# Parts of h, of the mixers' outputs and of the merged output at other places modulo 512 bytes

## The chip, the core and the metric

The kernel runs on one core of a Trainium2 chip, alone. The metric is the device time of one execution in microseconds, the median of several runs. A difference of two kernels is told as a ratio with its interval.

## What is computed

One decoder block on 256 positions of 2048 features, all float32: a normalised and modulated input, two causal mixers in parallel, a gated merge and an output projection.

```python
ada = c @ w_ada + b_ada
shift, scale, gate = jnp.split(ada, 3, axis=-1)
h = rms_norm(x, g_pre) * (1.0 + scale[:, None, :]) + shift[:, None, :]
proj = h @ w_in                                    # 2048 x 11824
(qa, kc, vc, ks, vs, kw, vw, ga, za, qb, kb, vb, zb, ma, mb) = jnp.split(proj, IN_SPLITS, axis=-1)
...
oa = nsa_attention(qa, ...)                        # 16 heads of 64, three branches
ya = (oa * jax.nn.silu(za)) @ w_br_a               # 1024 x 2048
...
ob = dilated_mixture(qb, kb, vb)                   # 8 heads of 128
yb = (ob * jax.nn.silu(zb)) @ w_br_b               # 1024 x 2048
merged = jax.nn.sigmoid(ma) * ya + jax.nn.sigmoid(mb) * yb
out = merged @ w_out                               # 2048 x 2048
return x + gate[:, None, :] * rms_norm(out, g_post)
```

## The kernel before, in words

Nearly all of the time goes into four products of float32 operands: h with w_in, the two mixers' outputs with w_br_a and w_br_b, and the merged output with w_out. Each is made of three products of parts. A float32 operand is split into a high part, rounded to fp32r, and a low part, the rest; the weights give wH and wL, h gives xH and xL, the mixers' outputs yH and yL, the merged output mH and mL. The product is high x high, high x low and low x high, summed in PSUM.

The weights come in items of up to 1024 columns per partition: one or two rows of 128 of the contraction (`kt`, 16 of them for h), 512 columns wide as a rule, 304 or 256 in a few panels. SP's queue loads an item into `raw` (seven buffers), ScalarE writes wH from it (L488), VectorE writes wL (L489), and TensorE multiplies. `items` is the order of the work, written out ahead: four passes over the panels of w_in as the rows of h become ready (PASSES and PIECES: row 0, rows 1 and 2, 3 to 6, 7 to 9, 10 to 12, 13 to 15), then the mixers' products and the output's. The attention of both mixers is a generator (`side_main`) of which a step is taken between items.

`product` (L528) issues an item's matmuls. For a panel as it is, the stationary operand is 128 columns (512 bytes per partition) of the h part and the moving operand the weights' 512 columns: for each of the item's rows L558 (xH with wH) and L559 (xL with wH), then for each row L561 (xH with wL), and the same for the second half of the positions. For the turned panels (za, zb) the weights are stationary and the h part, 256 columns, is moving: L548, L550, L553. The first pass uses unsplit float32 operands (L536, L540). Between these stand small matmuls of the attention and transposes; near the end two float32 rows of the gate are broadcast by products with a tile of ones, `ones_r` (L1146, L1147), and the compression of the first mixer takes loads of 128 and 64 columns in turn (L574, L575).

A tile's place in SBUF follows from the order in which the pools' tiles are made. The pool `const` comes first; a tile of 64 bytes that nothing uses (`align`) makes it end at a multiple of 512 bytes per partition. All tiles of the pools `big`, `wp` and most of `work` are multiples of 512 bytes long, so each begins at a multiple of 512: xH (16 rows in one tile), the six xL parts, the panels' tiles QA to ZB, whose places the mixers' outputs take over later, and the weights' tiles. mL takes the place of xH, the mH parts those of xL. Tiles of `const` begin anywhere at a multiple of 32: `ones_r` at 192 past a multiple of 512, VBD at 384.

Of the kernel before, what the change touches and what calls it, by code (L numbers as in the profile page):

```python
# [9 lines left out]
F32 = mybir.dt.float32  # L10
F32R = mybir.dt.float32r
BF = mybir.dt.bfloat16
I32 = mybir.dt.int32
AF = mybir.ActivationFunctionType
OP = mybir.AluOpType
# [3 lines left out]
S, D, N_IN = 256, 2048, 11824  # L19
KT = D // 128  # L20
# [6 lines left out]
PASSES = ((0, 1), (1, 3), (3, 7), (7, 16))  # L27
# [3 lines left out]
PIECES = (((1, 3),), ((3, 7),), ((7, 10), (10, 13)), ((13, 16),))  # L31
# [2 lines left out]
DA = (4, 6)  # L34
LAST = 3
ALIGN = 64
A_SCALE = 64 ** -0.5
B_SCALE = 128 ** -0.5

# [8 lines left out]
def _build(ctx, tc, x, c, positions, w_ada, b_ada, g_pre, g_post, w_in, pe_ck, pe_cv, w_ck1, w_ck2,  # L48
           w_cv1, w_cv2, w_br_a, w_br_b, w_out, out):
    nc = tc.nc  # L50
    V, A, T, G, DMA = nc.vector, nc.scalar, nc.tensor, nc.gpsimd, nc.sync
    const = ctx.enter_context(tc.tile_pool(name="const", bufs=1))
    big = ctx.enter_context(tc.tile_pool(name="big", bufs=1))
# [2 lines left out]
    psum = ctx.enter_context(tc.tile_pool(name="psum", bufs=1, space=PSUM))  # L56

    const.tile([128, ALIGN // 4], F32, name="align")

    def rows(ap2d, r0, nr, c0, n):  # L60
        return ap2d[r0 * 128:(r0 + nr) * 128, c0:c0 + n].rearrange("(a p) n -> p a n", p=128)
# [76 lines left out]
    rstd = const.tile([128, NT], F32)  # L138
    rsqrt(rstd, ssq, "x")

    xH = big.tile([128, KT, S], F32R, name="xH")
    hF = work.tile([128, PASSES[0][1], S], F32, name="hF", tag="PL", bufs=2)

    class Parts:

# [9 lines left out]
            tile_, a = self.at[k[1]]  # L155
            return tile_[k[0], k[1] - a, k[2]]

    groups = (PASSES[0],) + tuple(p for some in PIECES for p in some)
    xL, xT = Parts(), {}

    def lows(a, b, name, dt):
        return big.tile([128, b - a, S], dt, name=f"{name}{a}", tag=f"xL{a}")

    def x_norm(eng, a, b, t):
        xq = xs[:, t, a * 128:b * 128]
# [41 lines left out]
    AB = const.tile([128, 2, KT], F32)  # L207
# [10 lines left out]
    def make_h(a, b, acc):  # L218
        n = b - a
        if a:  # L220
            for half in range(2):
                ps = psum.tile([128, n, 128], F32, name="ada_ps", tag="pv")
                for j in range(n):
                    T.transpose(ps[:, j, :], acc[:, half, j * 128:(j + 1) * 128], ident)
                V.tensor_reduce(AB[:, half, a:b], ps, axis=AX.X, op=OP.add)
            V.tensor_tensor(AB[:, :, a:b], AB[:, :, a:b], bT[:, :, a:b], op=OP.add)
        else:
            V.tensor_tensor(AB[:, :, a:b], ada0[:, :, :, 0], bT[:, :, a:b], op=OP.add)
        V.scalar_tensor_tensor(AB[:, 1, a:b], AB[:, 1, a:b], 1.0, gT[:, a:b], op0=OP.add, op1=OP.mult)
        if a:  # L230
            h = ST[:, 2 + len(hxn) % 2].rearrange("p (k s) -> p k s", k=4)
        else:
            h = hF
        hxn.append(a)
        src = xT[a] if a else x0_ps
        if not a:
            for kt in range(b):
                ia = A.activation(xH[:, kt], src[:, kt], AF.Identity, scale=AB[:, 1, kt:kt + 1], bias=AB[:, 0, kt:kt + 1])
        for kt in range(a, b):
            V.tensor_scalar(h[:, kt - a], src[:, kt - a], AB[:, 1, kt:kt + 1], AB[:, 0, kt:kt + 1],  # L240
                            op0=OP.mult, op1=OP.add)
        if a:
            ia = A.activation(xH[:, a:b], h[:, :n], AF.Copy)
        low = lows(a, b, "xL", F32R)
        iv = V.tensor_tensor(low, h[:, :n], xH[:, a:b].bitcast(F32), op=OP.subtract)  # L245
        xL.put(low, a, b)
        return ia, iv

# [71 lines left out]
        tab["multB"], tab["maskB"], tab["keepC"], tab["maskC"], tab["blk"] = multB, maskB, keepC, maskC, blk  # L320


    QA = big.tile([128, NT, 1024], F32, name="QA", tag="qa")
    CV = big.tile([128, NT, 512], F32, name="CV", tag="cv")
    K2 = big.tile([128, NT, 4, 2, 64], F32, name="K2", tag="k2")
    VS = big.tile([128, NT, 256], F32, name="VS", tag="vs")
    VW = big.tile([128, NT, 320], F32, name="VW", tag="vw")
    ZA = big.tile([128, NT, 1024], F32, name="ZA", tag="za")
    QB = big.tile([128, NT, 1024], F32, name="QB", tag="qb")
    KB = big.tile([128, NT, 1024], F32, name="KB", tag="kb")  # L330
    VB = big.tile([128, NT, 1024], F32, name="VB", tag="vb")
    ZB = big.tile([128, NT, 1024], F32, name="ZB", tag="zb")
    MA = big.tile([128, NT, D], F32, name="MA", tag="ma")

    panels = []

# [364 lines left out]
    def side_main():  # L701
# [396 lines left out]

        while ("merged", 0) not in done:
            yield  # L1100
        mH, mL = Parts(), big.tile([128, KT, S], F32R, name="mL", tag="xH")
        for a, b in groups:
            mH.put(lows(a, b, "mH", F32R), a, b)
        yT["m"] = (mH, mL)
        for p in range(4):
            while ("merged", p) not in done:
                yield
            yield
            yield
            for t in range(NT):  # L1110
                ps = psum.tile([128, 4, 128], F32, name="m_ps", tag="pt")
                for j in range(4):
                    T.transpose(ps[:, j, :], MA[:, t, (4 * p + j) * 128:(4 * p + j + 1) * 128], ident)
                ts = slice(t * 128, (t + 1) * 128)
                for a, b in groups:
                    a, b = max(a, 4 * p), min(b, 4 * p + 4)
                    if a < b:
                        dH, o = mH.at[a]
                        A.activation(dH[:, a - o:b - o, ts], ps[:, a - 4 * p:b - 4 * p], AF.Copy, scale=0.5)
                        V.scalar_tensor_tensor(mL[:, a:b, ts], ps[:, a - 4 * p:b - 4 * p], 0.5,  # L1120
                                               dH[:, a - o:b - o, ts].bitcast(F32), op0=OP.mult, op1=OP.subtract)
                if t == NT - 1:
                    done.add(("mT", p))
                yield
# [105 lines left out]
```

## Time and profile before

| | |
|---|---|
| median of 3 runs | 824.94 us (823.79 to 826.5) |
| the profiled execution | 823.05 us |
| its span | 821.3 us |
| TensorE busy | 793.1 us, 97% |
| VectorE busy | 687.9 us, 84% |
| ScalarE busy | 417.7 us, 51% |
| GpSimd busy | 92.4 us, 11% |
| HBM read | 190.38 MB, 234 GB/s over the span |

The span is the time from the first to the last instruction of the profiled execution; its own time has a little before and behind it. Shares are of the span. In the rows PE is TensorE's matmuls, PEld its loads of stationary columns, DVE is VectorE, ACT ScalarE, POOL GpSimd. [...]

### The profile page before, as it was taken

The numbers are of one execution on the slowest core, as the hardware profiler recorded it, in microseconds if no ns is written. First come the engines' busy times: TensorE is split into PE (matmuls) and PEld (weight loads), VectorE is DVE, ScalarE is ACT, GpSimd is POOL, SyncE is SP. The second block draws the span as 40 slices with busy tenths as digits, with TensorE's granted clock in tenths as the row PEclk, the third lists the DMA queues.
The fourth block names the chain that finished last, engine by engine and source line by source line (L and its number), as shares of the span: only waits on it lengthen the run. The fifth ranks groups of instructions, "written<-read, shape, count | busy, mean of one in ns | idle before, by whom it ended". The sixth has DMA issues, their size and how long they took to land.

```text
span 821.3 us, 11929 instructions
## 1 busy us (share of the span) xinstructions
PE 793.1 (97%) x4160; PEld 667.3 (81%) x4160; DVE 687.9 (84%) x1068; ACT 417.7 (51%) x684; POOL 92.4 (11%) x111
## 2 busy tenths in 40 slices
PE   5999999999999999999999999999999999999995
PEld 4487888889887888888789999888887878888884
DVE  4799999999998879899888998867577999967455
ACT  2764263433434646566667666555644344445441
POOL 4200000000000026045412111001000010100000
PEclk9999999999999999999999999999999999999998
DMA  9899899999798547744444435655479999976533
GB/s 328 264 362 313 262 327 309 348 301 339 256 332 310 180 154 255 239 147 136 133 133 138 119 114 177 183 153 154 128 255 325 367 300 343 335 269 231 188 100 103
DMA packets 106950, 193.26 MB, mean 235 GB/s; under 512 B 7593, under 2 KB 36617, under 8 KB 106249
## 3 DMA queue, kind: packets, MB, share of 16 engines
q1 hardware_dynamic: 105376, 189.17, 69.5%
q10 hardware_dynamic: 1514, 3.33, 1.1%
q8 instruction: 33, 0.54, 0.3%
q14 instruction: 27, 0.22, 0.1%
HBM read 190.38 MB, written 2.10 MB: 234 GB/s over the span
## 4 chain that ended last, share of the span: by engine, by line
PE 85%; DVE 9%; issue 2%; DMA 2%; ACT 1%; DVEq 0%; ACTq 0%; SPq 0%
PE mm L558 21%; PE mm L561 21%; PE mm L559 21%; DVE wL L489 3%; PE mm L553 3%; PE mm L550 3%; PE mm L548 3%; PE mm L540 2%; DVE ST L509 2%; PE pt_ps L921 1%; PE sA L885 1%; PE ada_ps L183 1%; DMA xs<-in_x_dram 1%; DMA raw<-in_w_in_dram 1%; PE pvb_ps L1056 1%
## 5 line engine op out<-in xcount | busy, mean ns | idle before, releaser
L488 ACT ACTIVATE wH<-raw 128x1024 fp32r<-128x1024 f32 (+2 forms) x268 | 267.3, 1000 | 293.0 <-PE mm L559 182.3
L489 DVE TENSOR_TENSOR wL<-raw,wH 128x1024 fp32r<-128x1024 f32 (+2 forms) x268 | 316.4, 1185 | 74.1 <-ACT wH L488 69.2
L558 PE MATMUL mm<-wH,xH 128*128 128x512 f32 (+2 forms) x616 | 237.1, 387 | 1.3 <-DVE KB L631 1.1
L559 PE MATMUL mm<-wH,xL 128*128 128x512 f32 (+2 forms) x616 | 234.3, 382 | 0.0
L561 PE MATMUL mm<-wL,xH 128*128 128x512 f32 (+2 forms) x616 | 188.4, 383 | 0.4 <-DVE wL L489 0.4
L558 PEld LDWEIGHTS mm<-wH,xH 128*128 128x128 f32 x616 | 115.8, 188 | 23.0 <-issue 2.7
L559 PEld LDWEIGHTS mm<-wH,xL 128*128 128x128 f32 x616 | 115.9, 188 | 20.4 <-DVE xL L245 0.3
L561 PEld LDWEIGHTS mm<-wL,xH 128*128 128x128 f32 x616 | 113.1, 188 | 23.2 <-DVE wL L489 1.9
L509 DVE SCALAR_TENSOR_TENSOR ST<-raw,vecT,ST 128x768 f32<-128x768 f32 (+2 forms) x75 | 76.0, 1013 | 3.3 <-DMA raw<-in_w_ada_dram 3.1
L548 PE MATMUL mm<-xH,wH 128*128 128x256 f32 x240 | 63.5, 284 | 1.0 <-DVE VB L631 1.0
L550 PE MATMUL mm<-xL,wH 128*128 128x256 f32 x240 | 63.1, 283 | 0.0
L553 PE MATMUL mm<-xH,wL 128*128 128x256 f32 x240 | 50.0, 284 | 0.4 <-DVE wL L489 0.4
L558 PE MATMUL mm<-wH,yH 128*128 128x512 f32 x128 | 50.2, 392 | 0.0
L559 PE MATMUL mm<-wH,yL 128*128 128x512 f32 x128 | 50.0, 390 | 0.0
L558 PE MATMUL mm<-wH,mH 128*128 128x512 f32 x128 | 49.9, 390 | 0.0
L559 PE MATMUL mm<-wH,mL 128*128 128x512 f32 x128 | 49.9, 390 | 0.0
L548 PEld LDWEIGHTS mm<-xH,wH 128*128 128x128 f32 x240 | 45.9, 191 | 1.6 <-issue 1.6
L509 DVE SCALAR_TENSOR_TENSOR gacc<-raw,vecT,gacc 128x1024 f32<-128x1024 f32 x30 | 38.4, 1278 | 9.3 <-DMA raw<-in_w_ada_dram 9.3
L550 PEld LDWEIGHTS mm<-xL,wH 128*128 128x128 f32 x240 | 45.9, 191 | 0.0
L561 PE MATMUL mm<-wL,mH 128*128 128x512 f32 x128 | 39.8, 389 | 0.0
L561 PE MATMUL mm<-wL,yH 128*128 128x512 f32 x128 | 39.5, 390 | 0.0
L553 PEld LDWEIGHTS mm<-xH,wL 128*128 128x128 f32 x240 | 37.9, 192 | 0.8 <-DVE wL L489 0.8
(296 smaller groups left out, 1003.8 us busy)
## 6 DMA issues: line engine op xcount, KB each, us to landing
raw<-in_w_in_dram SPq DMA_DIRECT2D x165, 512.0 KB, 4.4
raw<-in_w_ada_dram SPq DMA_DIRECT2D x48, 512.0 KB, 5.5
raw<-in_w_ada_dram SPq DMA_DIRECT2D x48, 384.0 KB, 4.7
raw<-in_w_out_dram SPq DMA_DIRECT2D x32, 512.0 KB, 4.8
raw<-in_w_br_a_dram SPq DMA_DIRECT2D x16, 512.0 KB, 5.7
raw<-in_w_br_b_dram SPq DMA_DIRECT2D x16, 512.0 KB, 6.1
raw<-in_w_in_dram SPq DMA_DIRECT2D x29, 256.0 KB, 3.1
raw<-in_w_ada_dram SPq DMA_DIRECT2D x24, 256.0 KB, 4.9
```

What stands on the lines that cost most here:

```text
L183: T.matmul(ada0[:, half, j, :], lhsT=raws0[q][:, kk, half, j * 128:(j + 1) * 128], rhs=cT[:, kt:kt + 1].to_broadcast([128, 128]), start=(k ...
L488: A.activation(H, raw, AF.Copy)
L489: V.tensor_tensor(L, raw, H.bitcast(F32), op=OP.subtract)
L509: V.scalar_tensor_tensor(acc, r, cc, acc, op0=OP.mult, op1=OP.add)
L540: T.matmul(job.ps[t][:, :job.n], lhsT=hj[:, t * 128:(t + 1) * 128], rhs=it.raw[:, j, cs], start=(first and j == 0), stop=(last and j == it ...
L548: T.matmul(ps, lhsT=it.H[:, j, bs], rhs=sH[:, it.kt0 + j, :], start=(first and j == 0 and b == 0), stop=False, skip_group_check=True)
L550: T.matmul(ps, lhsT=it.H[:, j, bs], rhs=sL[:, it.kt0 + j, :], start=False, stop=False, skip_group_check=True)
L553: T.matmul(ps, lhsT=it.L[:, j, bs], rhs=sH[:, it.kt0 + j, :], start=False, stop=(last and j == it.nk - 1), skip_group_check=True)
L558: T.matmul(ps, lhsT=sH[:, it.kt0 + j, ts], rhs=it.H[:, j, cs], start=(first and j == 0), stop=False)
L559: T.matmul(ps, lhsT=sL[:, it.kt0 + j, ts], rhs=it.H[:, j, cs], start=False, stop=False)
L561: T.matmul(ps, lhsT=sH[:, it.kt0 + j, ts], rhs=it.L[:, j, cs], start=False, stop=(last and j == it.nk - 1))
L885: T.matmul(o, lhsT=QT[:, u.t, h // 2, h % 2, :], rhs=KTt[:, hl, :, 0:128] if u.t == 0 else KTt[:, hl, u.br, :], start=(hl == 0), stop=(hl ...
```

## The change

The single tile xH becomes six, one for each part of the rows of h, as xL was already; mL, which takes xH's place, likewise. `begin(offset)` makes an unused tile in the pool `big` that is just long enough for the next tile to begin `offset` bytes past a multiple of 512. Called ahead of each part it gives these places modulo 512:

| tiles | before | after |
|---|---|---|
| xH, xL, mH, mL, row 0 | 0 | 0 |
| rows 1 and 2 | 0 | 32 |
| rows 3 to 6 | 0 | 64 |
| rows 7 to 9 | 0 | 160 |
| rows 10 to 12 | 0 | 256 |
| rows 13 to 15 | 0 | 320 |
| QA, CV, K2, VS, VW, ZA, and in their places yH and yL of the second mixer, VR | 0 | 192 |
| QB, KB, VB, ZB, and in their places yH and yL of the first mixer | 0 | 224 |
| raw, wH, wL, and all else of `wp`, `work`; xs, MA, ST, AR, BS | 0 | 0 |

The unused tiles take 1536 bytes of each partition. The two programs have the same instructions with the same shapes in the same order on every engine, and each waits for the same; only addresses differ.

```diff
--- before.py
+++ after.py
@@ -34,6 +34,8 @@
 DA = (4, 6)
 LAST = 3
 ALIGN = 64
+OFFSETS = {0: 0, 1: 32, 3: 64, 7: 160, 10: 256, 13: 320}
+OFFSET_A, OFFSET_B = 224, 192
 A_SCALE = 64 ** -0.5
 B_SCALE = 128 ** -0.5
 
@@ -56,6 +58,15 @@
     psum = ctx.enter_context(tc.tile_pool(name="psum", bufs=1, space=PSUM))
 
     const.tile([128, ALIGN // 4], F32, name="align")
+    gaps = [0]
+
+    def begin(offset):
+
+        n = (offset - gaps[0]) % 512
+        if n:
+            big.tile([128, n // 4], F32, name=f"gap{len(gaps)}")
+            gaps.append(n)
+        gaps[0] = offset
 
     def rows(ap2d, r0, nr, c0, n):
         return ap2d[r0 * 128:(r0 + nr) * 128, c0:c0 + n].rearrange("(a p) n -> p a n", p=128)
@@ -138,8 +149,7 @@
     rstd = const.tile([128, NT], F32)
     rsqrt(rstd, ssq, "x")
 
-    xH = big.tile([128, KT, S], F32R, name="xH")
-    hF = work.tile([128, PASSES[0][1], S], F32, name="hF", tag="PL", bufs=2)
+    groups = (PASSES[0],) + tuple(p for some in PIECES for p in some)
 
     class Parts:
 
@@ -155,11 +165,31 @@
             tile_, a = self.at[k[1]]
             return tile_[k[0], k[1] - a, k[2]]
 
-    groups = (PASSES[0],) + tuple(p for some in PIECES for p in some)
+    def whole(name):
+        parts = Parts()
+        for a, b in groups:
+            if name == "xH":
+                begin(OFFSETS[a])
+            parts.put(big.tile([128, b - a, S], F32R, name=f"{name}{a}", tag=f"xH{a}"), a, b)
+        return parts
+
+    xH = whole("xH")
+    begin(0)
+    hF = work.tile([128, PASSES[0][1], S], F32, name="hF", tag="PL", bufs=2)
+
     xL, xT = Parts(), {}
 
+    seen = set()
+
     def lows(a, b, name, dt):
-        return big.tile([128, b - a, S], dt, name=f"{name}{a}", tag=f"xL{a}")
+        new = a not in seen
+        seen.add(a)
+        if new:
+            begin(OFFSETS[a])
+        part = big.tile([128, b - a, S], dt, name=f"{name}{a}", tag=f"xL{a}")
+        if new and b == KT:
+            begin(0)
+        return part
 
     def x_norm(eng, a, b, t):
         xq = xs[:, t, a * 128:b * 128]
@@ -235,14 +265,14 @@
         src = xT[a] if a else x0_ps
         if not a:
             for kt in range(b):
-                ia = A.activation(xH[:, kt], src[:, kt], AF.Identity, scale=AB[:, 1, kt:kt + 1], bias=AB[:, 0, kt:kt + 1])
+                ia = A.activation(xH[:, kt, :], src[:, kt], AF.Identity, scale=AB[:, 1, kt:kt + 1], bias=AB[:, 0, kt:kt + 1])
         for kt in range(a, b):
             V.tensor_scalar(h[:, kt - a], src[:, kt - a], AB[:, 1, kt:kt + 1], AB[:, 0, kt:kt + 1],
                             op0=OP.mult, op1=OP.add)
         if a:
-            ia = A.activation(xH[:, a:b], h[:, :n], AF.Copy)
+            ia = A.activation(xH.at[a][0], h[:, :n], AF.Copy)
         low = lows(a, b, "xL", F32R)
-        iv = V.tensor_tensor(low, h[:, :n], xH[:, a:b].bitcast(F32), op=OP.subtract)
+        iv = V.tensor_tensor(low, h[:, :n], xH.at[a][0].bitcast(F32), op=OP.subtract)
         xL.put(low, a, b)
         return ia, iv
 
@@ -320,17 +350,20 @@
         tab["multB"], tab["maskB"], tab["keepC"], tab["maskC"], tab["blk"] = multB, maskB, keepC, maskC, blk
 
 
+    begin(OFFSET_B)
     QA = big.tile([128, NT, 1024], F32, name="QA", tag="qa")
     CV = big.tile([128, NT, 512], F32, name="CV", tag="cv")
     K2 = big.tile([128, NT, 4, 2, 64], F32, name="K2", tag="k2")
     VS = big.tile([128, NT, 256], F32, name="VS", tag="vs")
     VW = big.tile([128, NT, 320], F32, name="VW", tag="vw")
     ZA = big.tile([128, NT, 1024], F32, name="ZA", tag="za")
+    begin(OFFSET_A)
     QB = big.tile([128, NT, 1024], F32, name="QB", tag="qb")
     KB = big.tile([128, NT, 1024], F32, name="KB", tag="kb")
     VB = big.tile([128, NT, 1024], F32, name="VB", tag="vb")
     ZB = big.tile([128, NT, 1024], F32, name="ZB", tag="zb")
     MA = big.tile([128, NT, D], F32, name="MA", tag="ma")
+    begin(0)
 
     panels = []
 
@@ -1098,7 +1131,7 @@
 
         while ("merged", 0) not in done:
             yield
-        mH, mL = Parts(), big.tile([128, KT, S], F32R, name="mL", tag="xH")
+        mH, mL = Parts(), whole("mL")
         for a, b in groups:
             mH.put(lows(a, b, "mH", F32R), a, b)
         yT["m"] = (mH, mL)
@@ -1117,7 +1150,7 @@
                     if a < b:
                         dH, o = mH.at[a]
                         A.activation(dH[:, a - o:b - o, ts], ps[:, a - 4 * p:b - 4 * p], AF.Copy, scale=0.5)
-                        V.scalar_tensor_tensor(mL[:, a:b, ts], ps[:, a - 4 * p:b - 4 * p], 0.5,
+                        V.scalar_tensor_tensor(mL.at[a][0][:, a - o:b - o, ts], ps[:, a - 4 * p:b - 4 * p], 0.5,
                                                dH[:, a - o:b - o, ts].bitcast(F32), op0=OP.mult, op1=OP.subtract)
                 if t == NT - 1:
                     done.add(("mT", p))
```

## Rows read from the trace of the kernel before

**Rows 1.** The page: busy us, share, instructions; TensorE's granted clock in 40 slices.
```profile
PE 793.1 (97%) x4160; PEld 667.3 (81%) x4160; DVE 687.9 (84%) x1068; ACT 417.7 (51%) x684; POOL 92.4 (11%) x111
...
PEclk9999999999999999999999999999999999999998
```

**Rows 2.** The page: the chain of work that ended last, by engine.
```profile
PE 85%; DVE 9%; issue 2%; DMA 2%; ACT 1%; DVEq 0%; ACTq 0%; SPq 0%
```

**Rows 3.** Groups by shape: out<-moving,stationary, count | busy us, mean ns | idle before.
```profile
L558 PE MATMUL mm<-wH,xH 128*128 128x512 f32 x556 | 220.4, 397 | 1.3 <-DVE KB L631 1.1
...
L548 PE MATMUL mm<-xH,wH 128*128 128x256 f32 x240 | 63.5, 284 | 1.0 <-DVE VB L631 1.0
```

**Rows 4.** Timeline of TensorE in the third pass: start us, us, operation.
```profile
301.55 0.39 PE L558 MATMUL mm<-wH,xH 128*128 128x512 f32 x1
...
305.63 0.39 PE L558 MATMUL mm<-wH,xH 128*128 128x512 f32 x1
```

**Rows 5.** Timeline of TensorE in a turned panel; ten matmuls are left out between.
```profile
501.72 0.28 PE L548 MATMUL mm<-xH,wH 128*128 128x256 f32 x1
...
503.04 0.28 PE L553 MATMUL mm<-xH,wL 128*128 128x256 f32 x1
```

**Rows 6.** Timeline, loads of 128 and 64 columns in turn; thirteen matmuls left out.
```profile
307.22 0.28 PE L574 MATMUL hid_ps<-wH,BS 128*128 128x256 f32 x1
...
308.86 0.28 PE L574 MATMUL hid_ps<-wH,BS 128*128 128x256 f32 x1
```

**Rows 7.** Timeline of the first pass's turned panels, and the group of their loads.
```profile
41.19 3.62 PE L536 MATMUL mm<-hF,raw 128*128 128x256 f32 x16
44.64 0.38 PE L224 MATMUL ada_ps<-ident,ST 128*128 128x128 f32 x2
...
L536 PEld LDWEIGHTS mm<-hF,raw 128*128 128x128 f32 x32 | 5.9, 190 | 1.1 <-issue 0.5
```

**Rows 8.** Groups of VectorE by shape: tiles that begin at 0 and at 384.
```profile
L631 DVE TENSOR_TENSOR KB<-mm,KB 128x512 f32<-128x512 f32 x12 | 7.9, 679 | 0.3 <-PE mm L561 0.3
...
L812 DVE TENSOR_TENSOR VBD<-vc_ps,blk 128x512 f32<-128x512 f32 x2 | 1.3, 680 | 0.0
```

**Rows 9.** Timeline of the panel of 304 columns; eleven matmuls left out.
```profile
141.03 0.30 PE L558 MATMUL mm<-wH,xH 128*128 128x304 f32 x1
...
142.71 0.30 PE L558 MATMUL mm<-wH,xH 128*128 128x304 f32 x1
```

**Rows 10.** Timeline around two gate broadcasts, matmuls, and two loads (PEld).
```profile
740.38 0.39 PE L558 MATMUL mm<-wH,mH 128*128 128x512 f32 x1
...
740.83 0.39 PE L558 MATMUL mm<-wH,mH 128*128 128x512 f32 x1
741.06 0.40 PE L1146 MATMUL g_ps<-gH,ones_r 128*128 128x512 f32 x1
...
741.99 0.39 PE L558 MATMUL mm<-wH,mH 128*128 128x512 f32 x1
...
742.66 0.40 PE L1147 MATMUL g_ps<-gL,ones_r 128*128 128x512 f32 x1
...
743.59 0.39 PE L558 MATMUL mm<-wH,mH 128*128 128x512 f32 x1
...
744.04 0.39 PE L558 MATMUL mm<-wH,mH 128*128 128x512 f32 x1
...
740.84 0.19 PEld L1146 LDWEIGHTS g_ps<-gH,ones_r 128*128 128x128 f32 x1
741.06 0.19 PEld L559 LDWEIGHTS mm<-wH,mL 128*128 128x128 f32 x1
```

**Rows 11.** Timeline of TensorE while attention is mixed in.
```profile
365.71 0.40 PE L558 MATMUL mm<-wH,xH 128*128 128x512 f32 x1
...
366.64 0.62 PE L561 MATMUL mm<-wL,xH 128*128 128x512 f32 x2
```

**Rows 12.** A stretch near the end: length, busy us of each engine, clock, DMA share.
```profile
760.00:800.00 40.00, 40.00 (x178) 33.14 (x177) 20.85 (x21) 19.77 (x25) 0.00 (x0) 1.00 0.46 146
```

## The prediction

> **What bounds the kernel now.** [...] The groups by shape show the stream: 556 matmuls each for L558, L559 and L561 with xH and xL at 512 columns, 240 each for the turned panels (L548, L550, L553) at 256 [rows 3]. With the mixers' and the merged operands the program has 2436 of 512 columns, 810 of 256 and 90 of 304, each with its own load of stationary columns: 3336 pairs.
>
> [...] From 301.55 to 305.63 us eighteen matmuls pass in 4.08 us: 226.7 ns each [rows 4]. At 256 columns eleven pass in 1.32 us, 120.0 ns each [rows 5]. [...] Where every other load has only 64 columns, fourteen matmuls of 256 take 1.64 us, 117.1 ns each [rows 6]: a quarter of the loaded columns less saves 2.9 ns, so a whole load costs about 11.6. [...] So the load and the moving stream, both read from SBUF, get in each other's way, at about 12 ns per load, 3336 x 12 = 40 us in all. That is the cost on which this change can act.
>
> **The change, part by part.** It moves no instruction: each engine has the same instructions with the same shapes and waits in the same order in both programs; only SBUF addresses differ. Before, every large tile begins at a multiple of 512 bytes, and since a stationary operand is 512 bytes wide, load and moving stream always begin at zero modulo 512. After, the weights still do, and the h, y and merged operands begin at 32, 64, 160, 192, 224, 256 or 320 past it. In 3264 of the 3336 pairs the two operands now stand apart.
>
> The side engines cost nothing. VectorE wrote VBD, which begins 384 bytes past a multiple of 512, in 680 ns for 128x512, and KB, which begins at zero, in 679 [rows 8]. The loads and stores whose place moves (about 260 on VectorE, 135 on ScalarE, 58 on GpSimd) keep their durations by that row, and only the matmuls are left.
>
> For these the trace has two rows with a nonzero place. The first is the item of 304 columns and two rows: its second row of weights begins 1216 bytes on, 192 past a multiple of 512, so the moving operand alternates between 0 and 192 against a load at zero. [...] The second is the gate broadcast, L1146 and L1147, whose stationary ones_r begins at 192, while its moving operand and all its neighbours are at zero. Before it the stream is in step: from 740.38 three matmuls take 0.68 us. From 741.06 four take 0.93 us, where 0.91 was due, though the load of the next one began on time, at 741.06 as well [rows 10]; then it is in step until 742.66, where the next such load stands, and again four take 0.93. From 743.59 two take 0.45, in step. A single load from another place throws the stream out of step, and finding it again costs 0.93 - 0.907 = 0.023 us. That is one change of place and one change back: about 11.5 ns per change.
>
> Counted over the dense matmuls in order, the place of the h operand against the weights' changes 541 times after the edit, because an item holds two of the 16 rows and several items (rows 0 and 1, 2 and 3, 6 and 7, 9 and 10, 12 and 13) span two parts. 541 x 11.5 ns = 6.2 us if each change costs that. Changes inside such an item follow each other after one or two matmuls, before the four are over, so the other way to count is by matmuls out of step: 666 within these items and some 130 x 4 behind them, at 23/4 = 5.8 ns each, 6.9 us. Against that, the stream is out of step already where attention is mixed in: from 365.71 four take 0.93 us [rows 11]; a change costs nothing new there. I take off about a quarter and keep **+5 us**, that is 823.05 + 5 = 828 on the profiled execution; on the median of 824.94, **830**.
>
> Bounds of this term: nothing (the 304-column row), and, if the stream never finds its step with operands apart, 5.8 ns on all 2436 wide matmuls, 14 us. Below nothing: whatever of the 12 ns per load goes away.
>
> **The rivals.** *The place does not matter* (time 825). [...] Against it: the two gate broadcasts, each with the same four late matmuls and no late load. They also differ from their neighbours in the tile that they write (g_ps), but the stream changes that with every item, without harm. [...]
>
> *Standing apart frees the load* (faster; this is the other side). The 12 ns may be paid because both operands begin at the same place modulo 512. If any place but zero avoids it, 3264 x 12 ns = 39 us go, 786. If one place in the list does, it decides by its share: 160, 256 and 320 carry 576 matmuls each, 7 us, 818; two of them 811. [...] For it: no row shows the other six places, and all 3336 loads now pay at the one place in use. It decides from the point at which about 430 loads are freed, which pays for the 5 us of lost step.
>
> *No step at all* (slower still): with operands apart the stream may never settle; 14 us, 839. [...]
>
> That the edit does not do what it says is excluded: the places of the built program are those of the list.
>
> **How the numbers follow.** A difference under 0.3%, 2.5 us, can't be told from none here. Lost step at each change, 830 (827.4 to 834): 0.34. No step at all, 834 to 842: 0.08. The place does not matter, 822.5 to 827.4: 0.33. Freed loads: 0.25, a little over half of it between 810 and 822.5, since one or two places are likelier than all. So faster 0.25, same 0.33, slower 0.42. The range 810 to 839 leaves out the far side of the freed loads (0.11) and the end of the no-step case (0.04), and holds some 0.85. The likeliest case has its own range, 827 to 834, beside it, as both signs carry weight.
>
> **What would show it.** In the changed kernel's trace the starts at one place: 226.7 ns in rows 7 and 8, 11, 14 and 15 of h, and 231 to 236 for about four matmuls behind each change, would confirm the lost step. A steady pace other than 226.7 at one place, which would stand out in the mixers' products (192 and 224 with no change for dozens of matmuls), would mean that the place itself sets the cost, and the sum above would be wrong in kind: below 226.7 the third case, above it the fourth. 226.7 through the mixed items too would be the second. The total of VectorE, ScalarE and GpSimd should stay as it is, and TensorE's clock too.

## The result and the profile after

The changed kernel takes 829.88 us (median of 5 runs, 828.9 to 831.23) against 825.69 us for the kernel before (5 runs, 823.79 to 826.5): slower, ratio 1.0074 with an interval of 1.0054 to 1.0095. The two medians alone are 4.2 us apart, a quotient of 1.0051, a little under the interval of the recorded ratio; in the 13 to 29 runs taken beside each batch of the experiments below the kernel before has medians of 823.3 to 824.3. The profiled execution has a span of 827.9 us, 6.6 more than before. One execution each of h_at_320 (991.8 us at a mean granted clock of 0.754, the one that was profiled) and of turned_320 (4520.5 us) stands far from all others of its kernel and is in no median below. The forecast of 830 us holds. The reason given for it does not: a change of place costs next to nothing (227.7 and 228.2 ns at the changes between 0 and 256 in one_part, 227.7 and 227.8 without one), and what sets the pace is where the two operands of a pair begin against each other (226.7 ns together, 233.3 with the weights alone moved in w_at_192).

The page of the kernel after, with the rows that answer to [rows 1] and [rows 2] (busy us, share, instructions; TensorE's granted clock in 40 slices; the chain of work that ended last by engine):

```profile
PE 799.4 (97%) x4160; PEld 664.4 (80%) x4160; DVE 689.4 (83%) x1068; ACT 417.5 (50%) x684; POOL 92.5 (11%) x111
...
PEclk9999999999999999999999999999999999999998
...
PE 77%; DVE 13%; DMA 5%; issue 2%; ACT 1%; DVEq 0%; ACTq 0%; SPq 0%
```

The count of instructions is the same, VectorE gained 1.5 us, ScalarE and GpSimd stand still, and the clock is granted as before. TensorE is busy 6.3 us longer, and still the largest share of the chain. The groups by shape, to hold against [rows 3] and [rows 8] (out<-moving,stationary, count | busy us, mean ns | idle before):

```profile
L591 PE MATMUL mm<-wH,xH 128*128 128x512 f32 x556 | 222.3, 401 | 1.3 <-DVE KB L664 1.0 <-ACT xH L273 0.3
...
L581 PE MATMUL mm<-xH,wH 128*128 128x256 f32 x240 | 62.7, 282 | 1.0 <-DVE VB L664 1.0
...
L664 DVE TENSOR_TENSOR KB<-mm,KB 128x512 f32<-128x512 f32 x12 | 7.9, 683 | 0.3 <-PE mm L594 0.3
...
L845 DVE TENSOR_TENSOR VBD<-vc_ps,blk 128x512 f32<-128x512 f32 x2 | 1.3, 680 | 0.0
```

L591 is the L558 of before, L581 the L548: the matmuls of 512 columns list 401 ns for 397, those of 256 list 282 for 284. So the wide ones became slower and the turned ones faster. The pace itself is read from starts: a listed 401 ns is longer than the 226.7 to 233.3 ns from one start to the next. In the timeline of TensorE (start us, us, operation) the mixers' products stand first, where every operand of one mixer keeps one place for 48 matmuls at a time: yH and yL of mixer A at 224, of mixer B at 192.

```profile
635.88 0.40 PE L591 MATMUL mm<-wH,yH 128*128 128x512 f32 x1
...
641.48 0.40 PE L591 MATMUL mm<-wH,yH 128*128 128x512 f32 x1
...
694.54 0.39 PE L592 MATMUL mm<-wH,yL 128*128 128x512 f32 x1
...
700.03 0.39 PE L592 MATMUL mm<-wH,yL 128*128 128x512 f32 x1
```

Twenty-four matmuls lie between the two rows of each pair. At 224 they take 5.60 us, 233.3 ns each; at 192 they take 5.49, 228.8 each. Before, the pace was 226.7 [rows 4]. There is no change of place in either stretch, and the stream never comes back to 226.7.

The narrower matmuls, eleven of the turned panel of [rows 5] and twelve of the panel of [rows 9], in the same timeline of the kernel after:

```profile
140.56 0.30 PE L591 MATMUL mm<-wH,xH 128*128 128x304 f32 x1
...
142.24 0.30 PE L591 MATMUL mm<-wH,xH 128*128 128x304 f32 x1
...
503.28 0.28 PE L581 MATMUL mm<-xH,wH 128*128 128x256 f32 x1
...
504.53 0.28 PE L586 MATMUL mm<-xH,wL 128*128 128x256 f32 x1
```

304 columns still take 140.0 ns. The turned panel went from 120.0 to 1.25 / 11 = 113.6 ns.

Where the time went, by the gaps between starts added up over the whole trace, from the 201st matmul on (the first 200 hold the waits of the start, of which the longest, for the DMA of g_pre, is 6.3 us before and 6.2 after): the matmuls of 512 columns, with the gaps behind them, took 560.3 us before and 570.3 after, +10.0; those of 256 and 304 columns took 114.4 and 113.1, -1.3; all others 77.8 and 77.7. Gaps under 243 ns behind a wide matmul, which hold no wait, had a mean of 227.8 ns (2306 of them) before and 232.3 (2315) after. The first 200 matmuls ended 1.9 us earlier than before, at 57.2 us for 59.1; in the kernels below this point lies between 57.0 and 58.5 (h_at_320 apart), so the profile of before was the late one, and this is not of the change. 10.0 - 1.3 - 0.1 - 1.9 = +6.7 us, which is the difference of the spans. Part of the 10.0 belongs to the same late start: three kernels below that keep the pace of before (one_part, h_at_256, turned_0) have their first 200 behind them at 57.9 to 58.1 and then take 561.8 to 562.2 us for the wide matmuls with their gaps. Against these three the change adds 8.1 to 8.5 us there, and 5.9 to 6.1 us to the span. The runs have it at 4.5 to 7.8 by the ratio's interval.

### The profile page after: what moved, and what is told of

The parts are those of the page before. It is cut to its first block, busy times and chain, and to the rows that moved or that the text cites. A ratio compares the mean times of both kernels' runs of the same rounds, so it can differ in the third digit from the quotient of the medians.

```text
span 827.9 us, 11929 instructions
## 1 busy us (share of the span) xinstructions
PE 799.4 (97%) x4160; PEld 664.4 (80%) x4160; DVE 689.4 (83%) x1068; ACT 417.5 (50%) x684; POOL 92.5 (11%) x111
## 4 chain that ended last, share of the span: by engine, by line
PE 77%; DVE 13%; DMA 5%; issue 2%; ACT 1%; DVEq 0%; ACTq 0%; SPq 0%
PE mm L592 20%; PE mm L591 20%; PE mm L594 20%; DVE wL L522 4%; DMA raw<-in_w_in_dram 3%; PE mm L586 3%; PE mm L583 3%; PE mm L581 3%; DVE ST L542 2%; PE pt_ps L954 1%; PE sA L918 1%; DMA xs<-in_x_dram 1%; ACT wH L521 1%; PE ada_ps L213 1%; PE pvb_ps L1089 1%
## 5 line engine op out<-in xcount | busy, mean ns | idle before, releaser
L591 PE MATMUL mm<-wH,xH 128*128 128x512 f32 (+2 forms) x616 | 239.0, 390 | 1.3 <-DVE KB L664 1.0
L594 PE MATMUL mm<-wL,xH 128*128 128x512 f32 (+2 forms) x616 | 190.5, 386 | 0.2 <-DVE wL L522 0.2
L591 PEld LDWEIGHTS mm<-wH,xH 128*128 128x128 f32 x616 | 115.7, 188 | 25.0 <-issue 2.5
L594 PEld LDWEIGHTS mm<-wL,xH 128*128 128x128 f32 x616 | 113.3, 188 | 24.6 <-DVE wL L522 0.7
L581 PE MATMUL mm<-xH,wH 128*128 128x256 f32 x240 | 62.7, 282 | 1.0 <-DVE VB L664 1.0
L591 PE MATMUL mm<-wH,yH 128*128 128x512 f32 x128 | 50.7, 396 | 0.0
L591 PE MATMUL mm<-wH,mH 128*128 128x512 f32 x128 | 50.6, 395 | 0.0
L581 PEld LDWEIGHTS mm<-xH,wH 128*128 128x128 f32 x240 | 45.2, 188 | 1.6 <-issue 1.6
```

Source lines behind the costliest of these rows:

```text
L581: T.matmul(ps, lhsT=it.H[:, j, bs], rhs=sH[:, it.kt0 + j, :], start=(first and j == 0 and b == 0), stop=False, skip_group_check=True)
L591: T.matmul(ps, lhsT=sH[:, it.kt0 + j, ts], rhs=it.H[:, j, cs], start=(first and j == 0), stop=False)
L594: T.matmul(ps, lhsT=sH[:, it.kt0 + j, ts], rhs=it.L[:, j, cs], start=False, stop=(last and j == it.nk - 1))
```

## The experiments

From here on the **relation** of a pair is the place at which its load (the stationary operand) begins, minus that of the moving operand under which it is read (that of the matmul which is listed as running when the load starts, as in [rows 10]), modulo 512 bytes. Theories: A, as forecast, a change of place costs about 11.5 ns. B, the place sets the pace, at each matmul. Within B: it is the operand's own place, or it is the relation. A stream of 512 columns is called in step at 226.7 ns. The ratio of each kernel is to the kernel before, run beside it.

**h_at_320: no change of place at all.** Against the kernel after:

```diff
-OFFSETS = {0: 0, 1: 32, 3: 64, 7: 160, 10: 256, 13: 320}
-OFFSET_A, OFFSET_B = 224, 192
+OFFSETS = {0: 320, 1: 320, 3: 320, 7: 320, 10: 320, 13: 320}
+OFFSET_A, OFFSET_B = 320, 320
```

> All parts of h, of the mixers' outputs and of the merged output begin at 320 modulo 512, the weights at zero: operands stand apart everywhere, and no change of place remains. If each change of place costs (the term of my prediction), the stream is in step: 226.7 ns per 512-column matmul, 120 per 256-column one, 825.7 us. If the place itself sets the pace, as the groups at 320 in the changed kernel suggest (233.2 ns at 512 columns, 115.4 at 256 in those pairs where the stationary begins 192 past the moving operand): 2346 x 5.5 ns = +13 us and 785 x -4.4 ns = -3.5 us, 835 us.

831.0 us (median of three; ratio 1.0088, 1.0057 to 1.0119); its trace is not read for the pace. The time alone is enough against A, which asked for 825.7: with every change of place taken from the wide pairs the cost did not fall. The 835 that B asked for was not reached either; w_at_192 shows why.

**all_at_64: everything away from zero, the weights too, nothing apart.** Against the kernel before:

```diff
-ALIGN = 64
+ALIGN = 128
```

> The kernel before with its unused tile 64 bytes longer: every large tile, weights included, begins at 64 modulo 512. If the place of one operand against the other counts: 226.7 ns, 825.7 us. If the distance of a tile's own beginning from a multiple of 512 counts: some 233 ns as at 64 in the changed kernel, +10 us or more, 836 us. If changes of place cost: 825.7 us.

825.12 us, ratio 1.0017 (1.0002 to 1.0032): at most 2.6 us, where the change under study costs 4.5 at least. Twenty-four matmuls of the mixers' products in its timeline:

```profile
633.27 0.39 PE L558 MATMUL mm<-wH,yH 128*128 128x512 f32 x1
...
638.71 0.39 PE L558 MATMUL mm<-wH,yH 128*128 128x512 f32 x1
```

5.44 / 24 = 226.7 ns. An operand's own place, tried at 64, costs nothing in the pace as long as both stand there together.

**w_at_192: only the weights move**, so the wide pairs have relation 320, the turned ones 192. Against the kernel before, with a tile behind it that gives later tiles their old places back:

```diff
+    work.tile([128, 80], F32, name="back", tag="back", bufs=1)
...
+    wp.tile([128, 48], F32, name="gap", tag="gap", bufs=1)
```

> h and all other parts at zero, wH and wL at 192 modulo 512. The places of the two operands against each other are those of the run with h at 320 (stationary minus moving is 320 in the wide panels, 192 in the turned ones). If only the relation counts: that run's paces (233 and 115 ns) and time, 835 us. If the stationary operand's own place counts: the wide panels, whose stationary h stays at zero, keep 226.7 ns, and only the turned panels change, 822 to 826 us. If changes cost: 825.7 us.

830.85 us, ratio 1.0074 (1.0051 to 1.0097), as slow as the change under study. The same twenty-four matmuls, timeline of this kernel:

```profile
635.51 0.39 PE L560 MATMUL mm<-wH,yH 128*128 128x512 f32 x1
...
641.11 0.39 PE L560 MATMUL mm<-wH,yH 128*128 128x512 f32 x1
```

5.60 / 24 = 233.3 ns, with h, y and merged at zero throughout. Together with all_at_64 this leaves the relation. It also shows A's failure in a clean profile: nothing changes place from pair to pair, and the wide stream is slow from one end to the other.

The time is 4 us under the 835 expected, and the gaps tell where that went. The wide ones without a wait grew from 227.8 to 233.3 ns, 13 us over 2397 of them. But the wide matmuls with all their gaps take 570.6 us, only 8.4 to 8.8 more than in one_part, h_at_256 and turned_0: beyond the pace their gaps hold 11.2 us of waiting here, and 15.7 to 16.1 there. That fits a stream that, being slower, reaches later what it waits for; it was not traced wait by wait. The matmuls of 256 and 304 columns give back another 2.0 us.

**scan_b: the other places.** Against the kernel after:

```diff
-OFFSETS = {0: 0, 1: 32, 3: 64, 7: 160, 10: 256, 13: 320}
-OFFSET_A, OFFSET_B = 224, 192
+OFFSETS = {0: 0, 1: 96, 3: 128, 7: 288, 10: 352, 13: 384}
+OFFSET_A, OFFSET_B = 480, 448
```

> As the changed kernel, with the places that it left out: 96, 128, 288, 352 and 384 for the rows of h and the merged operand, 480 and 448 for the mixers' outputs. If the place sets the pace, each has its own steady value at 512 and at 256 columns between 224 and 240 and between 112 and 122 ns, and the mixers' products (144 matmuls or more at one place) do not settle at 226.7: 827 to 836 us. If changes cost: 226.7 ns within each place, slower matmuls only behind a change, 830 us.

830.62 us, ratio 1.0074 (1.0048 to 1.01). Mixer A at 480 and mixer B at 448, timeline:

```profile
637.09 0.39 PE L591 MATMUL mm<-wH,yH 128*128 128x512 f32 x1
...
642.69 0.39 PE L591 MATMUL mm<-wH,yH 128*128 128x512 f32 x1
...
694.94 0.39 PE L592 MATMUL mm<-wH,yL 128*128 128x512 f32 x1
...
700.43 0.39 PE L592 MATMUL mm<-wH,yL 128*128 128x512 f32 x1
```

233.3 ns at 480 and 228.8 at 448: what 224 and 192 had given, 256 bytes further on. The means of the wide gaps without a wait, by relation, from this kernel and the one under study:

| relation | mean ns | relation + 256 | mean ns |
|---|---|---|---|
| 32 | 232.8 | 288 | 232.9 |
| 64 | 233.3 | 320 | 233.2 |
| 96 | 233.4 | 352 | 233.9 |
| 128 | 232.7 | 384 | 232.5 |
| 160 | 233.0 | | |
| 192 | 230.0 | 448 | 229.0 |
| 224 | 233.2 | 480 | 233.2 |

The table takes the gaps at which the place does not change. The mean of 230.0 at 192 hides two paces: mixer B's four stretches of 48 matmuls in the kernel under study run at 228.9 ns, but for the second, which runs at 233.3 at the very same places (at 448 all four run at 229.0):

```profile
670.61 0.40 PE L591 MATMUL mm<-wH,yH 128*128 128x512 f32 x1
...
676.21 0.40 PE L591 MATMUL mm<-wH,yH 128*128 128x512 f32 x1
```

Twenty-four matmuls take 5.60 us. So at 192 the relation takes the stream out of step, but does not alone fix the pace that it then has.

So it looked as if places count modulo 256. But 256 itself had shown 230.3 in the kernel after, and zero 231 there, between stretches at other places.

**one_part and h_at_256: is 256 as good as zero, and do changes between the two cost anything?** Against the kernel after, one_part and then h_at_256:

```diff
+OFFSETS = {0: 0, 1: 0, 3: 0, 7: 0, 10: 256, 13: 0}
+OFFSET_A, OFFSET_B = 0, 0
...
+OFFSETS = {0: 256, 1: 256, 3: 256, 7: 256, 10: 256, 13: 256}
+OFFSET_A, OFFSET_B = 256, 256
```

> Rows 10 to 12 of h and of the merged operand begin at 256 modulo 512, all other parts and all weights at zero. If the place sets the pace and the step is found again behind it: the stream returns to 226.7 ns within some five matmuls after each visit to those rows; 576 of 3336 pairs at 230 ns (396 of them wide) plus some 20 ns for each return, 826.5 to 828.5 us. If each change of place costs 11.5 ns and the place nothing: 226.7 ns inside rows 10 to 12 as soon as four matmuls have passed. If once apart the stream stays out of step: 231 ns in the other rows too, 830 us or more.

> All parts of h, of the mixers' outputs and of the merged output at 256, weights at zero. If the relation counts modulo 256: as before, 226.7 and 120 ns, 824 us. If it counts modulo 512 and the run with one part at 256 only kept a step found at zero: 230 ns at 512 columns as at 256 in the changed kernel, 828 to 830 us.

one_part: 824.17 us, ratio 1.0003 (0.9986 to 1.0021). h_at_256: 823.59 us, ratio 1.0000 (0.9988 to 1.0011). Timelines, one_part in the output's product where items pass between 0 and 256, then h_at_256 in the mixers':

```profile
760.01 0.39 PE L592 MATMUL mm<-wH,mL 128*128 128x512 f32 x1
...
765.45 0.39 PE L592 MATMUL mm<-wH,mL 128*128 128x512 f32 x1
```

```profile
633.11 0.39 PE L591 MATMUL mm<-wH,yH 128*128 128x512 f32 x1
...
638.55 0.39 PE L591 MATMUL mm<-wH,yH 128*128 128x512 f32 x1
```

Both are 24 matmuls in 5.44 us, 226.7 ns. one_part has 167 changes of place among its wide pairs; the gaps at them average 227.7 and 228.2 ns, those without a change 227.7 and 227.8. Theory A asked for 11.5 more. Modulo 256 holds for the wide stream at every place tried, and the 230.3 of relation 256 in the kernel after came from its neighbours, not from its place. h_at_256 is also the control for the edit itself: it has the six tiles in place of one and the unused tiles, and takes the time of the kernel before.

**one_part_64: the same changes, to a place that is not a multiple of 256.** One number differs from one_part:

```diff
-OFFSETS = {0: 0, 1: 0, 3: 0, 7: 0, 10: 256, 13: 0}
+OFFSETS = {0: 0, 1: 0, 3: 0, 7: 0, 10: 64, 13: 0}
```

> The run with one part at 256, with that part at 64 instead: the same changes of place at the same matmuls, only the place differs. If the relation modulo 256 sets whether the stream can be in step: 230 to 236 ns in the wide matmuls of rows 10 to 12, four or five late ones behind each visit, then 226.7 again; 396 x 5 ns = 2 us plus some 1.5 us behind the visits, 826.5 to 828.5 us, where 256 gave 824.2. If that run was in step because one part in six is too little to lose it: 226.7 here too, 824 us.

824.55 us, ratio 1.0024 (1.0008 to 1.0039); its span is 823.8 us for one_part's 821.8. The time is 2 us under the range expected, the paces are those expected. This kernel shows both effects side by side, in the third pass where rows 10 to 12 end and row 13 begins:

```profile
299.71 0.39 PE L591 MATMUL mm<-wH,xH 128*128 128x512 f32 x1
...
302.04 0.63 PE L594 MATMUL mm<-wL,xH 128*128 128x512 f32 x2
...
303.20 0.39 PE L592 MATMUL mm<-wH,xL 128*128 128x512 f32 x1
...
305.24 0.39 PE L591 MATMUL mm<-wH,xH 128*128 128x512 f32 x1
```

From 299.71 to 302.04 ten matmuls take 2.33 us, 233 each: at relation 64 the pace stays there and does not recover. The second matmul of the row at 302.04 starts at 302.27 and reads under it the first load at zero again. From there four matmuls take 0.93 us, the very figure of the gate broadcasts [rows 10], and then nine take 2.04, 226.7 each. So a return to zero costs some 0.02 us, and staying at 64 costs over 6 ns on every matmul. Where an item mixes 64 and zero, the returns come before the four are over, and the zero pairs pay as well: the 83 wide gaps at a change back to zero average 232.3 ns, the 298 at 64 without a change 233.4.

**low_at_64: as many changes as can be made.** Only xL and the mH parts stand at 64; xH, mL and y at zero. Against the kernel after:

```diff
+OFFSETS = {0: 64, 1: 64, 3: 64, 7: 64, 10: 64, 13: 64}
+OFFSET_A, OFFSET_B = 0, 0
...
-                begin(OFFSETS[a])
+                begin(0)
```

> Only the tiles that lows() makes (xL, and mH, which takes their places) begin at 64, everything else at zero; every third load stands apart, and the place changes with nearly every matmul. If a change costs 11.5 ns: some 2000 changes, +20 us, 845 us. If the place sets the pace and only pairs that stand apart pay: a third of the wide matmuls at 233, +5 us, 829 us. If one load apart is enough to keep the stream out of step: all wide matmuls between 230 and 236 ns, 832 to 836 us.

827.3 us, ratio 1.0042 (1.0024 to 1.0059), with some 2000 changes by the count that gave the forecast its 541, more than three and a half times as many, and a little over half of the cost. In the output's product, where the two places alternate:

```profile
763.61 0.39 PE L591 MATMUL mm<-wH,mH 128*128 128x512 f32 x1
...
767.79 0.39 PE L591 MATMUL mm<-wH,mH 128*128 128x512 f32 x1
```

18 matmuls in 4.18 us, 232.2 ns each, a change at two of three: not more than a steady place apart costs. In this product two of three loads stand apart (mH), with h only every third (xL); yet the wide gaps average 231.3 ns over the h products too, and those at a return to zero 232.5. So pairs at zero pay with their neighbours, as the last of the three cases had it: the next visit comes before four matmuls have passed. The time stayed under all three cases.

**y_at_224: the price of one place by itself**, h and merged at zero:

```diff
+OFFSETS = {0: 0, 1: 0, 3: 0, 7: 0, 10: 0, 13: 0}
+OFFSET_A, OFFSET_B = 224, 224
```

> h and the merged operand at zero; only the panels' tiles, and in their places the mixers' outputs, begin at 224. The 768-column share of the stream is 384 wide matmuls in one stretch with no change of place among them. If the place sets the pace: 233 ns there against 226.7, 384 x 6.5 ns = 2.5 us, 826.3 to 828 us, and 226.7 elsewhere. If changes cost: 226.7 ns everywhere, 823.8 us. The other engines' work on these tiles (attention, rotary, gates) adds nothing in either.

825.34 us, ratio 1.0014 (1.0000 to 1.0028), 1 us under the range expected. The wide gaps at 224 average 233.3 ns, all others 227.9. 377 gaps at 5.4 ns more are 2.0 us, and the span, at 824.1, lies 2.1 above h_at_256's. Runs alone would hardly tell so much from nothing.

**turned_0, turned_192, turned_320: can the faster turned panels be had alone?** The weights' tiles are made 128 columns longer, and the turned panels' weights begin 0, 192 or 320 bytes into them. To make room, one tile of `const` moves into `work` and a pool of four buffers has three (turned_0 is the control with that alone):

```diff
+            o = 48 if it.kind == "w" and it.jobs[0].turned else 0
-            H, L = (wp.tile([128, 1024], F32R, name="w" + x, tag="w" + x, bufs=3)[:, :it.nk * it.n].rearrange(
+            H, L = (wp.tile([128, 1152], F32R, name="w" + x, tag="w" + x, bufs=3)[:, o:o + it.nk * it.n].rearrange(
```

(48 words for turned_192; 0 and 80 in the other two.)

> A control for the next two runs: the kernel before, with wH and wL tiles 512 bytes longer (a tile of the identity's making and one of four rotary buffers give up their room), all operands at zero as before. 120 ns at 256 columns, 226.7 at 512; within 0.3% of the kernel before.

> As the control, but in the turned panels (za, zb: the weights are stationary, h moves) the weights lie 192 bytes into their longer tiles; the wide panels keep every operand at zero. If a pair's own place sets its pace: wide matmuls in step at 226.7, the 720 turned ones at 115 to 117 ns as in the two runs that had this relation, 720 x 3 to 4.5 ns = 2 to 3.3 us less than the control, 0.3 to 0.4% faster than the kernel before. If places apart only cost: as the control or slower.

> As the run with 192, with the weights of the turned panels 320 bytes into their tiles. The narrow panel of 256 columns ran at 115.1 ns at this relation with the weights shifted, the turned ones at 117.8 in the changed kernel with h at 192 or so; 115 to 118 ns expected, 1.5 to 3.5 us less than the control if a pair's own place sets its pace, nothing if places apart only cost.

824.2 us (ratio 0.9998, 0.9981 to 1.0015), 823.11 us (0.9985, 0.9971 to 1.0000) and 823.41 us (median of eleven; 0.9994, 0.9977 to 1.0011). The panel of [rows 5] in turned_0, then in turned_320:

```profile
500.85 0.28 PE L549 MATMUL mm<-xH,wH 128*128 128x256 f32 x1
...
502.17 0.28 PE L554 MATMUL mm<-xH,wL 128*128 128x256 f32 x1
```

```profile
499.41 0.28 PE L549 MATMUL mm<-xH,wH 128*128 128x256 f32 x1
...
500.66 0.28 PE L554 MATMUL mm<-xH,wL 128*128 128x256 f32 x1
```

Eleven take 1.32 us, 120.0 ns each, and 1.25 us, 113.6. Over the trace the gaps of 256 columns that hold no wait have a mean of 119.8 ns in turned_0, 117.2 at 192 and 115.4 at 320: over some 700 of them about 1.9 and 3.0 us saved. The wide ones keep their 227.8. The means are again mixtures of two paces. turned_192 runs two stretches of its turned panels, with the same places, like this:

```profile
473.14 0.28 PE L549 MATMUL mm<-xH,wH 128*128 128x256 f32 x1
...
477.22 0.28 PE L549 MATMUL mm<-xH,wH 128*128 128x256 f32 x1
...
490.68 0.28 PE L549 MATMUL mm<-xH,wH 128*128 128x256 f32 x1
...
494.92 0.28 PE L549 MATMUL mm<-xH,wH 128*128 128x256 f32 x1
```

Thirty-six matmuls take 4.08 us in the first, 113.3 ns each, and 4.24 in the second, 117.8. At 320 more of the stretches run at 113.3.

But the time does not follow clearly: the interval of turned_320 leaves no room for 3 us, that of turned_192 has room for its 1.9. The turned panels run among the attention, where TensorE waits for VectorE. Its waits from 430 to 500 us, turned_0, then turned_320 (engine line waited for: us in total, times, longest):

```profile
PE pt_ps L922 <- DVE AR L848: 0.7, 1, 0.7
PE pt_ps L922 <- DVE AR L834: 0.5, 1, 0.5
```

```profile
PE pt_ps L922 <- DVE AR L848: 1.0, 1, 1.0
PE pt_ps L922 <- DVE PL L927: 0.9, 1, 0.9
PE pt_ps L922 <- DVE AR L834: 0.6, 1, 0.6
PE pt_ps L922 <- DVE CS L871: 0.2, 1, 0.2
```

1.5 us more of waiting for producers that are no earlier: the waits of L922 for AR end 0.9 us sooner in turned_320, whose 201st matmul starts 1.0 us sooner. Half of the gain of 3.0 us ends there. In this profile the rest, and more, is lost later, between the mixers' products. Timeline of turned_320, and its stretch 665.0 to 668.5 us (length, busy us of each engine, granted clock, DMA share):

```profile
663.83 0.63 PE L1114 MATMUL m_ps<-ident,MA 128*128 128x128 f32 x4 [3.06 <-DVE mL L1121]
...
665.32 0.63 PE L559 MATMUL mm<-wH,yH 128*128 128x512 f32 x1
665.74 0.63 PE L560 MATMUL mm<-wH,yL 128*128 128x512 f32 x1
```

```profile
665.00:668.50 3.50, 3.50 (x10) 2.71 (x9) 3.37 (x7) 1.60 (x3) 0.00 (x0) 0.51 0.87 313
```

TensorE came earlier to the transposes of L1114 and sat idle 3.06 us until VectorE had written mL (2.17 in turned_0, where the clock stays at 1.00). Behind this idle time the granted clock read 1.00 from 664.0 to 665.0 us and 0.51 from 665.0 to 668.5, and from 665.32 on the matmuls start 0.42 us apart: seven gaps each 0.20 us longer than turned_0's, 1.4 us gone. From its 201st matmul to its last turned_320's profile is 2.1 us longer than turned_0's; -3.0 + 1.5 + 0.9 + 1.4 make 0.8 of that, and the other 1.3 were not followed. The medians of the runs differ by 0.8 us the other way, which is within their intervals. The fall of the clock was seen in one profile. The other runs have no trace; a mean granted clock as low as the profile's, 0.995 or less, stands on record for eight of the eleven of turned_320 and for three of the twelve of turned_0, which fits such a fall in them and does not show it. No version here beats both kernels beyond the measurement; turned_192, at 0.9985, comes nearest.

## Why the prediction was right in its number and wrong in its reason

**What bounds the kernel** was right: TensorE's pace per matmul decided, at an unchanged clock (39 of the 40 slices read 9 and the last reads 8, before and after) and with side engines at next to nothing, as [rows 8] had promised (KB 683 ns, VBD 680 after).

**The step that failed is "a change of place costs 11.5 ns".** Its row was sound, and its reading was not. [rows 10] showed one load at 192 followed by loads at zero, and the stream four matmuls out of step. I read the loss as the price of changing and the recovery as finding the step at a place, any place. one_part_64 shows what the recovery was: the return to zero. At 64 there is none. Changes between places that both keep the step cost nothing (one_part), and without any change the cost is whole (h_at_320, w_at_192). The 541 changes therefore were the wrong thing to count. The right count was of wide pairs whose operands stand apart modulo 256, with the few at zero that follow each return (232.5 ns in low_at_64).

**"No step at all" was the right rival in kind**, and got 0.08. What stood against it was the 304-column row [rows 9], from which the prediction also has the "nothing" among the bounds of its term. That this row, at 192, lost nothing was the author's estimate; no run shows what 304 columns take without a load. It still reads 140.0 ns after, with other places, so it never had anything to say on 512 columns. The widths differ in sign: wide pairs lose apart (226.7 to 233.3 ns), turned ones of 256 gain (120.0 to 113.6), 304 does neither (140.0 in both kernels). A row of another width was carried over as if the cost were the load's alone.

**Why 830 and not that rival's 839.** Its price was 5.8 ns on 2436 wide matmuls, 14 us. Measured were 4.5 ns on the gaps without a wait, 227.8 to 232.3, some 10.7 us over the 2397 behind the first 200 matmuls: less than 5.8, because relation 192 costs less than half in three stretches of four (228.9 ns, where 224 takes 233.3), and because pairs at 256 were seen back in step behind their first four matmuls (rows 10 and 11 in a panel of the last pass: 2.26 us for the ten from 602.88 to 605.14, 226 ns each). Of these 10.7, 2 to 3 us came back as shorter waits, as the 8.1 to 8.5 against the three kernels at the old pace show. The turned panels gave 1.3 back, which no case had. The forecast of +5 came out because 541 changes at 11.5 ns, with a quarter taken off, happen to make a similar sum; the agreement is luck and says nothing for the term.

**"The place does not matter"** fell with the 226.7 against 233.3 ns of w_at_192.

**"Standing apart frees the load"**, the faster side, holds for matmuls of 256 columns alone: 120.0 to 113.3 ns at best (turned_192), 6.7 of the 12 ns that the prediction puts on a load. Those 12 are its estimate from [rows 5] and [rows 6], four times the 2.9 ns between 120.0 and 117.1; another estimate, from [rows 4] and [rows 5], takes the 106.7 ns between 226.7 and 120.0 for the time of 256 columns and leaves 13.3 over them. No run shows a stream without loads. It was looked for in the wide stream, where every relation tried that is no multiple of 256 costs (means of 229.0 to 233.9 ns, for 227.8 before). The forecast's own test, a steady pace other than 226.7 in the mixers' products, was the right one, and it decided.

**Left open.** Why 256 bytes: no run shows what in the reading of the two operands repeats with it. Places finer than 32 bytes were not tried. Why 256 columns gain is open too. And out of step the relation is not the whole of it, at either width: the panel of [rows 5] runs at 113.4 ns in w_at_192 and at 117.8 in turned_192, both with weights at 192 and h at zero, turned_192 alone holds both paces, and at 512 columns relation 192 holds 228.9 and 233.3. What chooses between the two was not found.

## What to carry to other kernels

Where a stream of wide matmuls has a load for each, let the loaded and the moving operand begin at the same place modulo 256 bytes; in this kernel that is worth up to 6.6 ns of 227 on every wide pair, some 13 us where all stand apart (w_at_192), of which about half shows in the time. It is the difference of the two places that counts, not their alignment: 226.7 ns with both at 64 (all_at_64), 233.3 with the weights alone at 192 (w_at_192). When a trace shows a single disturbed spot, it can't tell whether a change or a state is paid for: look for, or make, a stretch that holds the state before counting either. A saving ahead of a wait for another engine is not a saving, and a loss ahead of one is not a whole loss: in turned_320 the turned panels became 3 us faster and the kernel not measurably so, and in w_at_192 shorter waits, 11.2 us for 15.7 to 16.1, took up a good part of the 13 us.

## What the runs showed of the hardware that was not expected

- The pace of fp32r matmuls of 512 columns, each with a load of 128 columns: 226.7 ns at relations 0 and 256, 228.8 at 192 and 448 (233.3 in one of the four stretches at 192), 233.3 in steady stretches at 224, 320 and 480; at 32, 64, 96, 128, 160, 288, 352 and 384 the means lie between 232.5 and 233.9.
- Matmuls of 256 columns go the other way: 120.0 ns at relation zero, and at relation 192 or 320 steady stretches of either 113.3 or 117.8, both within turned_192. Those of 304 columns take 140.0 in both kernels.
- Behind a load from elsewhere the wide stream was back at 226.7 ns after four matmuls, 0.93 us for 0.907, at the gate broadcasts and in one_part_64. In both the load had returned to relation zero; while it stood at 64 the stream did not get back.
- TensorE's granted clock read 0.51 from 665.0 to 668.5 us, behind an idle stretch of 3.06 us, in turned_320, and 1.00 behind one of 2.17 us in turned_0. That cost 1.4 us, more than the 0.9 by which the wait had grown.
